# A hybrid decoder block on one core: a new order of the blocks where the MLP's first product begins, two loads moved in the DMA queue, and one place of weight preparation in attention

## The chip, the core and the metric

The kernel runs on 1 core of one Trainium2 chip. The core has TensorE (PE) for matmuls, which writes to PSUM banks of 128 x 512 f32; VectorE (DVE) and ScalarE (ACT) for elementwise work; GpSimd (POOL); and SyncE (SP), whose queue issues nearly all DMAs of this kernel. Each engine works through its own instructions in the order in which the program lists them, and waits on semaphores for the others. The metric is the device time in microseconds, the median of several runs. Before the change it is 2211.28 us.

## What is computed

A decoder block on x (1 x 1024 x 1024, f32): two parallel token mixers (retention, and dilated sliding-window attention in three groups of four heads), gates, and an MLP, each behind an RMS norm that is modulated by a condition; then a final norm.

```python
def squared_relu_mlp(h, w1, w2):
    return jnp.square(jax.nn.relu(h @ w1)) @ w2

def reference(x, c, w_ada, ...):
    for l in range(DEPTH):
        mod = jax.nn.silu(c) @ w_ada[l] + b_ada[l]
        sh1, sc1, g1, sh2, sc2, g2 = jnp.split(mod, 6, axis=-1)
        h = modulate(rms_norm(x, norm1_g[l]), sh1, sc1)
        x = x + g1[:, None, :] * token_mixer(h, w_in[l], ...)
        h = modulate(rms_norm(x, norm2_g[l]), sh2, sc2)
        x = x + g2[:, None, :] * squared_relu_mlp(h, w_ff1[l], w_ff2[l])
    return rms_norm(x, norm_f_g)
```

D_MODEL is 1024, the MLP is 4096 wide, a head has 128 channels.

## The kernel before

**Numbers.** Every f32 operand of a matmul is split into a high part (a copy by ScalarE into the matmul's type, names ending in h) and a low part (the rest, a subtraction by VectorE, names ending in l). A product is then three matmuls: low x high (L207), high x low (L209), high x high (L211), added up in one bank (mm3).

**Large products** run as 2 x 2 blocks with seven products in place of eight (class Blocks). The names of the seven in the first MLP product are 11, 12, s1, s3, s2, 22, s4; each is 12 matmuls of 128 x 512. The operands of x are 11, 21, 22 (the quarters) and t1 to t4 (their sums and differences, OPERAND). A tile pair q, of which there are NQ = 16, needs seven blocks (q, n) and four PSUM banks: bank 0 takes 11, then 12 on top of it; bank 1 takes s1, then s4; bank 2 takes s2; bank 3 takes s3, then 22. What has to be known of its methods:

- prep(q, n) makes a block's weight: for n = s1, s2, s3, s4 first a sum on VectorE (L249), then the high half on ScalarE (L254). The low half on VectorE (L264) is put off until the next prep or a flush. A weight needs a slot; most slots come back when the block's matmuls are done.
- mm(q, n) issues the 12 matmuls, and flushes the low half first if it is still open.
- post(q, n) works on the results. post(q, 11) copies bank 0 into a tile u (L286). post(q, s2) is three subtractions on VectorE: u - bank 2 (L290), v = bank 3 - u (L291), and v - bank 1 as output 22 (L1997); each output is followed by ReLU and square on ScalarE (L1998, L1999). So s4 (bank 1) and 22 (bank 3) of a q can start only behind its post(q, s2). post(q, 12), (q, 22), (q, s4) give outputs 11, 21, 12; with 21 and 12 a row of outputs is stored (f_out).
- run takes a list of blocks and issues for each: mm, then preps of coming weights as far as slots are free, a flush, post. For blocks that count as ahead (s2) post comes before the preps.

**The entry (ff1).** Half of x is normalized and split while the last steps of w_o run; so the blocks 11 of q = 0, 1 can start at once. The other half is normalized here (norm, L2047, on VectorE, with the row factors n21rb that come through TensorE), and the operands follow one after the other: t1 (L2065, then x_split, L2035 and L2036), 22 (L2038, L2039), t3 (L2079), t2 (L2088), t4 (L2105). On TensorE the blocks run (0, 11), (1, 11), (0, 12), (1, 12), (0, s1), (1, s1), (0, s3), (1, s3), (0, s2), (1, s2), and then, through run, (0, s4), (1, s4), (0, 22), (1, 22), and all blocks of q = 2, 3, and so on. a_sums (L2014 to L2019) builds two more sums of a finished q on VectorE, each pair with a store (xs_d), which the second product reads. Raw weights of q + 2 are loaded ahead of (q, 11) (w1_load).

**The second product (ff2_blocks)** goes through SEQ, seven block names for each of three chunks. Block i needs two operand tiles that b_load(i) reads back from DRAM (L2198, names b{i}0l and b{i}1l) and b_x(i, j) splits (L2184, L2180). b_load(0) is issued at (15, 11). b_load(1) is issued at the end of (15, 22), behind the store of that block's output; b_load(2) at the start of ff2_blocks, behind two loads of x1.

**Attention.** Steps has the weights of a step prepared while earlier steps run: following(s) takes what is missing of step s + 1 and the weight of step s + 2, and each preparation releases a load in SyncE's queue. A step that isn't marked manual calls following ahead of its own body. att_step(pair, i) computes keys (ak, gen runs over k = 0 to 7) and weaves something else in. For pair 1, i = 0 this is the last product of pair 0 (weave_pv): transposes of the probabilities on TensorE (L1435), their high half on ScalarE (L1439, pth) and low half on VectorE (L1440, ptl), then matmuls pv (L1459, L1460, L1461).

Of the kernel before, what the change touches and what calls it, by code (L numbers as in the profile page):

```python
# [17 lines left out]
P = 128  # L18
# [122 lines left out]
def block_kernel(ctx, tc, io, stop=None, dbg=None):  # L141
# [84 lines left out]
    class Blocks:  # L226
# [54 lines left out]
        def post(self, q, n):  # L281

            a, d, b, c = self.ps[q]
            if n == "11":
                self.t[q] = self.temps(f"{self.name}t{q}")
                nc.scalar.copy(self.t[q][0], a)  # L286
                return
            u, v = self.t[q]
            if n == "s2":
                nc.vector.tensor_sub(u, u, b)  # L290
                nc.vector.tensor_sub(v, c, u)  # L291
# [8 lines left out]
        def run(self, items, sums, before=lambda q, n: None, after=lambda q, n: None, ahead=(), rate=lambda q: 9):  # L300

            items_ahead = lambda i: i + 1 < len(items) and items[i + 1][1] in ahead
            for i, (q, n) in enumerate(items):
                before(q, n)
                self.mm(q, n)
                if n in ahead:
# [7 lines left out]
                if n not in ahead:  # L316
                    self.post(q, n)
                after(q, n)

# [626 lines left out]
        t = x4(name)  # L946
        return t.rearrange("p (a b) -> p a b", a=2)

    def a_temps(name):
        t = a_two(name)  # L950
        return t[:, 0], t[:, 1]

    def a_out(q, n, x, y=None):

# [45 lines left out]
    def queries_keys(ahead):  # L1000
        for _ in range(4):
            copy_block()
        sums = [(q, n) for q in range(NA) for n in ORDER][4:]

        def before(q, n):
            if n == ORDER[0] and q + 2 < NA:
                for part in (1, 2):
                    a_load(q + 2, part)

        turns = []  # L1010

# [20 lines left out]
        BA.run([(q, n) for q in range(NA) for n in ORDER], sums, before, after, ("s2",), lambda q: 1 if q == 0 else 2)  # L1032
        while turns:
            drain(turns.pop())
        values(ahead)
# [490 lines left out]
    def att_step(pair, i):  # L1526

        g, a = combos[i]

        def body(*args):  # L1530
            ps = ps_mm(f"ak{pair}{i}")
            gen = with_sums(proj_gen(ps, args[-1]))
            if i == len(combos) - 2:
                v_fetch(pair, 0)
            if i > 0:
                last = combos[i - 1]
                weave(gen, NK, scores_gen(pair, *last), len(SB[last[0]]), lag=2)
# [24 lines left out]
        return body  # L1562
# [319 lines left out]
    def norm_acc(x, f, key, pool):  # L1882

        n = x.shape[1]
        if f == 0:
            acc = pool.tile([P, 512], F32, tag="nacc", bufs=2, name=f"acc{key}")[:, :n]
            nc.scalar.activation(acc, x, AF.Square)
            G["acc", key] = acc
        else:
            sq = pool.tile([P, 512], F32, tag="nsq", bufs=2, name=f"sq{key}{f}")[:, :n]  # L1890
# [91 lines left out]
    def f_sums(name):  # L1982
        return G["mp"].tile([P, 2, 512], F32, tag="rl", bufs=2, name=name)

    def f_temps(name):
        return [G["mp"].tile([P, 512], F32, tag=t, bufs=2, name=name + t) for t in ("nsq", "h2t")]

    def f_out(q, n, x, y=None):

# [51 lines left out]
    def ff1(ahead):  # L2041
# [13 lines left out]
        G["rb"] = rstd_bcast(G["rs"], 0, 4, "n21")  # L2055
        BF.mm(1, "11", range(2, 4))
        BF.post(1, "11")
        BF.prep((2, "s3"))
        BF.mm(0, "12")
        BF.mm(1, "12")  # L2060
        low = None
        for m in range(4):
# [5 lines left out]
            low = x_split("t1", m, t1, None, "mh", 32)  # L2068
        norm(1)
        low()  # L2070
        BF.mm(0, "s1")
        BF.mm(1, "s1")
        lows = []
        for m in range(4):
            if m > 0:
# [6 lines left out]
            low = x_split("t3", m, t3, G["p"], "g1", 8)  # L2082

        def t2(m):
            k = 2 * m + 1
            t = t_(k, 1)
            lows[m]()
            nc.vector.scalar_tensor_tensor(t, t, mods[:, SH2 + k:SH2 + k + 1], t_(2 * m, 0), op0=ALU.add, op1=ALU.add)  # L2088
            return x_split("t2", m, t, G["p"], "g1", 8)

        for m in range(4):
# [3 lines left out]
            if m == 0:  # L2095
                BF.mm(0, "s3")
                BF.mm(1, "s3")
        low()
        BF.mm(0, "s2")
        BF.mm(1, "s2")  # L2100

        def t4(m):
            k = 2 * m + 1
            t = t_(k, 0)
            nc.vector.scalar_tensor_tensor(t, t, mods[:, SH2 + k:SH2 + k + 1], t_(k, 1), op0=ALU.add, op1=ALU.subtract)  # L2105
# [14 lines left out]
        for q in (3, 4):  # L2120
            for part in (1, 2):
                w1_load(q, part)
        for q in range(2):
            BF.post(q, "12")
        sums = [(q, n) for q in range(2, NQ) for n in ORDER]
        items = [(q, n) for n in ("s4", "22") for q in range(2)] + sums

        def before(q, n):
            if q > 2 and n == ORDER[0] and q + 2 < NQ:
# [3 lines left out]
                for f in range(3):  # L2133
                    x1_load(f + 3 * (n == "12"), x1_d)

        late = {(0, "22"): (0, 0), (2, "11"): (0, 1), (2, "12"): (1, 0), (2, "22"): (1, 1)}
        late.update({(q + 1, n): (q, part) for q in range(2, 4 * NS) for part, n in enumerate(("11", "s1"))})

        def after(q, n):
            if (q, n) in late:  # L2140
# [105 lines left out]
    def second_ahead(n):  # L2246
# [14 lines left out]
        elif n == "12":  # L2261
            for p in range(4):
                b_w(1, p)
        elif n == "22":
            b_load(1)

    def ff2_blocks(ahead):
        for i, (c, n) in enumerate(SEQ):
            if i == 0:
                b_load(2)  # L2270
                for s in range(2):
                    b_raw(0, "12", s)
            if i + 3 < len(SEQ) + 2:
# [280 lines left out]
```

## Time and profile before

| | us |
|---|---|
| median of 3 runs | 2211.28 |
| lowest and highest of them | 2211.12, 2213.42 |
| the profiled execution | 2211.89 |
| its span, from first to last instruction | 2210.1 |

So 1.8 us of the profiled execution lie around its span. The mean granted TensorE clock is 0.998. Three places of the span matter here, in us from its start: the step of attention about 1113 to 1133, the entry of the MLP from 1563 to 1650, and the beginning of the second product from 1878 to 1905.

In the timeline a row has the start, the duration, the engine, the line, the operation, the tile written, the tiles read, the shapes, and the count of instructions that were merged into the row; brackets give the engine's idle time ahead of it and what ended it. Matmuls are pipelined: their durations overlap, and what counts is the distance from start to start. Instructions of VectorE and ScalarE overlap a little too. In the view of waits a row says which engine and line waited for which engine, tile and line: us in total, how many times, the longest.

### The profile page before, as it was taken

The page shows a single profiled execution, that of the slowest core. Times are in us where ns is not written, and L with a number is a line of the kernel's source. Part 1 is how long each engine was busy: PE and PEld are TensorE (multiplying, and loading weights), DVE is VectorE, ACT ScalarE, POOL GpSimd, SP SyncE. Part 2 cuts the span into 40 slices and gives each one's busy share as a digit, 9 for nine tenths or more (in the row PEclk, how much of TensorE's full clock was granted, in tenths as well). Part 3 has the DMA queues.
Part 4 walks back from the last instruction along what each step waited for, and adds up shares of the span by engine and source line. Part 5 has one row for each costly group of instructions (what it writes and reads, how often), then busy time and mean ns, then how long its engine had stood idle before and what let it go on. Part 6 is the DMA issues. An engine that isn't in the chain of part 4 may idle for free. (4 is left out here: it accounts for less than half of the span.)

```text
span 2210.1 us, 27246 instructions
## 1 busy us (share of the span) xinstructions
PE 2174.1 (98%) x10134; PEld 1802.7 (82%) x10134; DVE 1456.5 (66%) x2284; ACT 921.8 (42%) x1689; POOL 161.0 (7%) x192
## 2 busy tenths in 40 slices
PE   7999999999999999999999999999999999999998
PEld 5888888888887888888888888888778888788887
DVE  6618777764548778865554754676876665787845
ACT  4323332223334445544644634524454445533413
POOL 0001111000012122111100000002000000000003
PEclk9999999999999999999999999999999999999999
DMA  9539999635776556557763265655244444745322
GB/s 366 201 133 280 301 289 291 193 112 181 237 269 199 176 176 206 195 169 193 175 167 96 87 252 176 239 181 161 67 159 151 146 146 183 253 134 173 122 86 77
DMA packets 156611, 408.93 MB, mean 185 GB/s; under 512 B 27446, under 2 KB 55357, under 8 KB 153278
## 3 DMA queue, kind: packets, MB, share of 16 engines
q1 hardware_dynamic: 148542, 363.14, 46.7%
q0 software_dynamic: 7936, 44.05, 9.2%
q8 instruction: 80, 1.31, 0.2%
q14 instruction: 53, 0.43, 0.1%
HBM read 316.27 MB, written 156.13 MB: 214 GB/s over the span
## 5 line engine op out<-in xcount | busy, mean ns | idle before, releaser
L207 PE MATMUL qap<-hh,qaw 128*128 128x512 f32 x216 | 84.0, 389 | 0.0
L209 PE MATMUL qap<-hl,qaw 128*128 128x512 f32 x216 | 84.0, 389 | 0.0
L211 PE MATMUL qap<-hh,qaw 128*128 128x512 f32 x216 | 84.0, 389 | 0.0
L634 POOL TENSOR_TENSOR j<-qk,j 128x512 fp32r<-128x512 f32 x32 | 43.3, 1353 | 460.5 <-ACT j L633 441.6
L1998 ACT ACTIVATE a<-a 128x512 f32<-128x512 f32 x48 | 30.3, 632 | 76.0 <-DVE a L1997 76.0
L1895 POOL TENSOR_TENSOR accnf<-accnf,sqnf 128x256 f32<-128x256 f32 (+1 forms) x18 | 16.6, 922 | 613.3 <-ACT sqnf L1891 613.3
L264 DVE TENSOR_TENSOR fw<-w1r,fw 128x512 fp32r<-128x512 f32 x48 | 32.9, 688 | 37.5 <-ACT fw L254 37.5
L1315 ACT ACTIVATE P<-P,ng 128x128 f32<-128x128 f32 (+1 forms) x96 | 42.0, 439 | 36.7 <-DVE ng L1312 36.7
L264 DVE TENSOR_TENSOR qaw<-wa,qaw 128x512 fp32r<-128x512 f32 x54 | 36.0, 685 | 30.8 <-ACT qaw L254 30.8
L2184 ACT CAST w2h<-w2s 128x512 fp32r<-128x512 f32 x36 | 22.4, 622 | 78.8 <-DVE w2s L2222 77.0
L207 PE MATMUL fp<-h2h,fw 128*128 128x512 f32 x128 | 50.0, 390 | 0.0
L209 PE MATMUL fp<-h2l,fw 128*128 128x512 f32 x128 | 49.8, 389 | 0.0
L211 PE MATMUL fp<-h2h,fw 128*128 128x512 f32 x128 | 49.8, 389 | 0.0
L207 PE MATMUL roa<-rh,rwl 128*128 128x512 f32 x128 | 49.8, 389 | 0.0
L209 PE MATMUL roa<-rl,rwh 128*128 128x512 f32 x128 | 49.8, 389 | 0.0
L211 PE MATMUL roa<-rh,rwh 128*128 128x512 f32 x128 | 49.8, 389 | 0.0
L1730 DVE TENSOR_TENSOR rwl<-rwl,rwh 128x1024 fp32r<-128x1024 f32 x25 | 30.2, 1220 | 29.1 <-ACT rwh L1760 29.1
L669 ACT COPY sm<-sT 128x128 f32<-128x128 f32 x32 | 8.5, 267 | 93.9 <-PE sT L657 93.9
L207 PEld LDWEIGHTS qap<-hh,qaw 128*128 128x128 f32 x216 | 40.5, 188 | 8.5
L209 PEld LDWEIGHTS qap<-hl,qaw 128*128 128x128 f32 x216 | 40.5, 188 | 8.4
L211 PEld LDWEIGHTS qap<-hh,qaw 128*128 128x128 f32 x216 | 40.5, 188 | 8.4
L1895 POOL TENSOR_TENSOR accn<-accn,sqn 128x512 f32<-128x512 f32 x12 | 15.5, 1294 | 392.3 <-ACT sqn L1891 392.3
(3100 smaller groups left out, 7213.6 us busy)
## 6 DMA issues: line engine op xcount, KB each, us to landing
v<-vd SPq DMA_DIRECT2D x32, 512.0 KB, 5.3
raw<-in_w_ada_dram SPq DMA_DIRECT2D x32, 512.0 KB, 4.8
w1r<-in_w_ff_dram SPq DMA_DIRECT2D x32, 512.0 KB, 5.0
vd<-vo SPq DMA_DIRECT2D x24, 512.0 KB, 6.5
yt<-y POOLq DMA_DIRECT2D x24, 512.0 KB, 6.9
xsd<-as SPq DMA_DIRECT2D x24, 512.0 KB, 2.7
w2r<-in_w_ff2s_dram SPq DMA_DIRECT2D x24, 512.0 KB, 6.9
em<-in_w_ada_dram SPq DMA_DIRECT2D x16, 512.0 KB, 10.2
```

The lines of the kernel that those rows point to most:

```text
L207: nc.tensor.matmul(o, wl, xh, start=first, stop=False, skip_group_check=skip)
L209: nc.tensor.matmul(o, wh, xl, start=False, stop=False, skip_group_check=skip)
L211: nc.tensor.matmul(o, wh, xh, start=False, stop=last, skip_group_check=skip)
L264: nc.vector.tensor_sub(t[:, 512:], src, fv(t[:, :512]))
L634: nc.gpsimd.tensor_sub(t[:, 1], src, fv(t[:, 0]))
L669: nc.scalar.copy(sm, ps[:, :C])
L1315: nc.scalar.activation(v, v, AF.Exp, bias=ng[:, blk:blk + 1], accum_out=st[:, g, blk, 2 + a:3 + a])
L1730: nc.vector.tensor_sub(lo, fv(lo), fv(hi))
L1895: (nc.vector if f == 7 else nc.gpsimd).tensor_add(G["acc", key], G["acc", key], sq)
L1998: nc.scalar.activation(o, o, AF.Relu)
L2184: nc.scalar.copy(hi, src)
```

## The change

Four edits.

1. In attention the first step of pair 1 is marked late: following isn't called ahead of its body but behind its fourth k.
2. The entry of the MLP has a new order on TensorE: ... (1, 12), (2, 11), (0, s1), (1, s1), (2, 12), (0, s3), (1, s3), (0, s2), (1, s2), (0, s4), (1, s4), (2, s1), (2, s3), (0, 22), (1, 22), (2, s2), (3, 11), (2, 22), (2, s4), (3, s1) and on as before. Nine banks would be in use, so bank 0 of q = 0, and later that of q = 2, is copied to a tile f11 by ScalarE. u has three buffers in place of two, and the tiles of post are taken one at a time. The weight of (2, 12) is prepared with that of (2, s3), ahead of the normalizations.
3. On VectorE, in the entry, t2 is built in the place of t1 and not in that of 22, so that the low halves of 22 can come behind t2, among t4 and the posts. post(0, 12) and post(1, 12) move, (q, 22) of q = 0, 1 counts as ahead, a_sums of q = 0, 1, 2 and b_load(1) go through a new hook, between, which stands behind the preps and ahead of flush and post.
4. b_load(1) is issued ahead of the store of (15, 22); b_load(2) directly behind the last block of the first product, ahead of the two loads of x1.

The diff, cut to its core:

```diff
-        def run(self, items, sums, before=..., after=..., ahead=(), rate=lambda q: 9):
+        def run(self, items, sums, before=..., after=..., ahead=lambda q, n: False,
+                rate=lambda q: 9, between=lambda q, n: None):
...
                     self.prep(sums.pop(0))
+                between(q, n)
                 if not items_ahead(i):
                     self.flush()
...
-                gen = at(gen, NK - 1, lambda: k_split(pair, g, a, ps))
+                gen = at(at(gen, 3, args[0]), NK - 1, lambda: k_split(pair, g, a, ps))
                 weave_pv(gen, NK - 1, 0, 2)
...
-                      manual=i == pair == 0)
+                      manual=("late" if pair else True) if i == 0 else False)
...
-        BF.prep((2, "s3"))
+        BF.prep((2, "s3"), (2, "12"))
         BF.mm(0, "12")
+
+        t = G["mp"].tile([P, 512], F32, tag="f11", name="f11")
+        nc.scalar.copy(t, BF.ps[0][0])
+        BF.ps[0][0] = t
         BF.mm(1, "12")
...
+        BF.mm(2, "11")
+        BF.post(2, "11")
         BF.mm(0, "s1")
         BF.mm(1, "s1")
+        BF.mm(2, "12")
...
         def t2(m):
-            k = 2 * m + 1
-            t = t_(k, 1)
-            lows[m]()
-            nc.vector.scalar_tensor_tensor(t, t, mods[:, SH2 + k:SH2 + k + 1], t_(2 * m, 0), op0=ALU.add, op1=ALU.add)
+            t = t_(2 * m, 0)
+            nc.vector.scalar_tensor_tensor(t, t_(2 * m + 1, 1), mods[:, SH2 + 2 * m + 1:SH2 + 2 * m + 2], t,
+                                           op0=ALU.add, op1=ALU.add)
...
+        lows[0]()
         low()
         BF.mm(0, "s2")
         BF.mm(1, "s2")
...
+        lows[1]()
         low = t4(0)
+        lows[2]()
+        low()
+        lows[3]()
         BF.post(0, "s2")
-        low()
         low = t4(1)
         BF.post(1, "s2")
         low()
+        BF.post(1, "12")
...
-        for q in range(2):
-            BF.post(q, "12")
-        sums = [(q, n) for q in range(2, NQ) for n in ORDER]
-        items = [(q, n) for n in ("s4", "22") for q in range(2)] + sums
+        BF.post(0, "12")
+        t = G["mp"].tile([P, 512], F32, tag="f11", name="f11b")
+        nc.scalar.copy(t, BF.ps[2][0])
+        BF.ps[2][0] = t
+        sums = [(q, n) for q in range(2, NQ) for n in ORDER if (q, n) not in ((2, "11"), (2, "12"))]
+        first_items = [(0, "s4"), (1, "s4"), (2, "s1"), (2, "s3"), (0, "22"), (1, "22"), (2, "s2"), (3, "11")]
+        items = first_items + [i for i in sums if i not in first_items]
...
-        late = {(0, "22"): (0, 0), (2, "11"): (0, 1), (2, "12"): (1, 0), (2, "22"): (1, 1)}
-        late.update({(q + 1, n): (q, part) for q in range(2, 4 * NS) for part, n in enumerate(("11", "s1"))})
+        late = {(0, "22"): (0, 0), (1, "22"): (0, 1), (2, "22"): (1, 0), (2, "s4"): (1, 1), (3, "s1"): (2, 0), (3, "s3"): (2, 1)}
+        late.update({(q + 1, n): (q, part) for q in range(3, 4 * NS) for part, n in enumerate(("11", "s1"))})
+
+        def between(q, n):
+            if q < 3 and (q, n) in late:
+                a_sums(*late[q, n])
+            if (q, n) == (2, "22"):
+                BF.post(2, "12")
+            if (q, n) == (NQ - 1, "22"):
+                b_load(1)
...
-        BF.run(items, sums[3:], before, after, ("s2",))
+        BF.run(items, sums[2:], before, after, lambda q, n: n == "s2" or n == "22" and q < 2,
+               lambda q: 1 if q == 2 else 9, between)
+        b_load(2)
         x1_load(6, x1_d)
         x1_load(7, x1_d)
...
-        elif n == "22":
-            b_load(1)
...
             if i == 0:
-                b_load(2)
                 for s in range(2):
                     b_raw(0, "12", s)
```

More of the change, by code (lines that the diff above doesn't have):

```diff
@@ L284, in post @@
             if n == "11":
-                self.t[q] = self.temps(f"{self.name}t{q}")
+                self.t[q] = [self.temps(f"{self.name}t{q}", 0)]
                 nc.scalar.copy(self.t[q][0], a)
                 return
-            u, v = self.t[q]
+            if n == "s2":
+                self.t[q].append(self.temps(f"{self.name}t{q}", 1))
+            u, v = self.t[q][0], self.t[q][-1]
             if n == "s2":
@@ L298, in post, with run @@
                 self.out(q, "12", u, d)
-        def run(self, items, sums, before=lambda q, n: None, after=lambda q, n: None, ahead=(), rate=lambda q: 9):
-            items_ahead = lambda i: i + 1 < len(items) and items[i + 1][1] in ahead
+        def run(self, items, sums, before=lambda q, n: None, after=lambda q, n: None, ahead=lambda q, n: False,
+                rate=lambda q: 9, between=lambda q, n: None):
+            items_ahead = lambda i: i + 1 < len(items) and ahead(*items[i + 1])
             for i, (q, n) in enumerate(items):
@@ L307, in run @@
                 self.mm(q, n)
-                if n in ahead:
+                if ahead(q, n):
                     self.post(q, n)
@@ L313, in run @@
                     self.prep(sums.pop(0))
+                between(q, n)
                 if not items_ahead(i):
                     self.flush()
-                if n not in ahead:
+                if not ahead(q, n):
                     self.post(q, n)
@@ L947, in a_two, with a_temps @@
         return t.rearrange("p (a b) -> p a b", a=2)
-    def a_temps(name):
-        t = a_two(name)
-        return t[:, 0], t[:, 1]
+    pairs = {}
+    def a_temps(name, i):
+        if i == 0:
+            pairs[name] = a_two(name)
+        return pairs[name][:, i]
     def a_out(q, n, x, y=None):
@@ L1030, in after @@
                 v_low(0, int(n == "22"))
-        BA.run([(q, n) for q in range(NA) for n in ORDER], sums, before, after, ("s2",), lambda q: 1 if q == 0 else 2)
+        BA.run([(q, n) for q in range(NA) for n in ORDER], sums, before, after, lambda q, n: n == "s2", lambda q: 1 if q == 0 else 2)
         while turns:
@@ L1983, in f_sums, with f_temps @@
         return G["mp"].tile([P, 2, 512], F32, tag="rl", bufs=2, name=name)
-    def f_temps(name):
-        return [G["mp"].tile([P, 512], F32, tag=t, bufs=2, name=name + t) for t in ("nsq", "h2t")]
+    def f_temps(name, i):
+        t = ("nsq", "h2t")[i]
+        return G["mp"].tile([P, 512], F32, tag=t, bufs=3 - i, name=name + t)
     def f_out(q, n, x, y=None):
@@ L2104, in t4 @@
             t = t_(k, 0)
-            nc.vector.scalar_tensor_tensor(t, t, mods[:, SH2 + k:SH2 + k + 1], t_(k, 1), op0=ALU.add, op1=ALU.subtract)
+            nc.vector.scalar_tensor_tensor(t, t, mods[:, SH2 + k:SH2 + k + 1], t_(2 * m, 0), op0=ALU.add, op1=ALU.subtract)
             return x_split("t4", m, t, A["r1"], "att", 8)
+        lows[1]()
         low = t4(0)
+        lows[2]()
+        low()
+        lows[3]()
         BF.post(0, "s2")
-        low()
         low = t4(1)
@@ L2134, in before @@
                     x1_load(f + 3 * (n == "12"), x1_d)
-        late = {(0, "22"): (0, 0), (2, "11"): (0, 1), (2, "12"): (1, 0), (2, "22"): (1, 1)}
-        late.update({(q + 1, n): (q, part) for q in range(2, 4 * NS) for part, n in enumerate(("11", "s1"))})
+        late = {(0, "22"): (0, 0), (1, "22"): (0, 1), (2, "22"): (1, 0), (2, "s4"): (1, 1), (3, "s1"): (2, 0), (3, "s3"): (2, 1)}
[7 more added lines that the diff above has]
+                b_load(1)
         def after(q, n):
-            if (q, n) in late:
+            if q > 2 and (q, n) in late:
                 a_sums(*late[q, n])
```

2 lines of the change are left out of this document (1 added, 1 removed).

## The prediction

> **What bounds the kernel now.** I read the page first, then TensorE's waits, the windows around the three places that the change touches, and the timelines there.
>
> ```profile
> PE 2174.1 (98%) x10134; PEld 1802.7 (82%) x10134; DVE 1456.5 (66%) x2284; ACT 921.8 (42%) x1689; POOL 161.0 (7%) x192
> ```
> ```profile
> PE fp L209 <- DVE xt L2036: 3.7, 4, 1.1
> ...
> PE fp L207 <- DVE ft2h2t L291: 1.5, 1, 1.5
> PE pv L1460 <- DVE ptl020(0, 0, 0)_9394 L1440: 1.2, 1, 1.2
> ...
> PE f2c L209 <- DVE b10l L2180: 0.8, 1, 0.8
> ...
> PE f2a L209 <- DVE b21l L2180: 0.4, 1, 0.4
> ```
> ```profile
> 1118.00:1126.00 8.00, 6.75 (x31) 5.36 (x30) 3.76 (x6) 2.00 (x4) 0.84 (x1) 0.79 0.91 329
> 1577.00:1605.00 28.00, 24.28 (x101) 17.86 (x100) 27.22 (x42) 14.11 (x23) 0.00 (x0) 1.00 0.21 72
> ...
> 1630.00:1650.00 20.00, 20.00 (x89) 16.30 (x88) 15.03 (x25) 9.32 (x16) 0.00 (x0) 1.00 0.55 197
> ```
>
> TensorE is busy for 98% of the span and the change takes no matmul away, so only its waits can be won. Five of them lie where the change is: two in the MLP's entry (3.7 and 1.5 us), one in attention (1.2), two where the second product begins (0.8 and 0.4). The windows (columns: length, busy time of PE, PEld, DVE, ACT, POOL, granted clock, DMA share, GB/s) add two facts: VectorE works 27.22 of 28 us in the entry, so there its queue sets the pace; and in attention the clock falls, to 0.79 on average, right at the wait.
>
> **Attention.** Rows of step 0 of pair 1:
>
> ```profile
> 1115.68 1.21 DVE L198 TENSOR_TENSOR raw_8741l<-raw,raw_8741h 128x1024 fp32r<-128x1024 f32 x1
> 1115.98 1.04 ACT L1252 ACTIVATE qh<-raw 128x1024 fp32r<-128x1024 f32 x1
> ...
> 1116.92 1.04 ACT L197 CAST raw_9294h<-raw 128x1024 fp32r<-128x1024 f32 x1
> ...
> 1117.05 1.23 DVE L1253 SCALAR_TENSOR_TENSOR ql<-raw,qh 128x1024 fp32r<-128x1024 f32 x1 [0.16 <-ACT qh L1252]
> ...
> 1117.86 0.58 ACT L1439 CAST pth020(0, 0, 0)_9393<-pt020(0, 0, 0)_9388 128x512 fp32r<-128x512 f32 x1
> ...
> 1118.19 1.22 DVE L198 TENSOR_TENSOR raw_9294l<-raw,raw_9294h 128x1024 fp32r<-128x1024 f32 x1
> ...
> 1118.49 0.33 PE L1459 MATMUL pv<-pth020(0, 0, 0)_9393,vl 128*128 128x128 f32 x1
> ...
> 1119.33 0.68 DVE L1440 TENSOR_TENSOR ptl020(0, 0, 0)_9394<-pt020(0, 0, 0)_9388,pth020(0, 0, 0)_9393 128x512 fp32r<-128x512 f32 x1
> ...
> 1120.07 0.33 PE L1460 MATMUL pv<-ptl020(0, 0, 0)_9394,vh 128*128 128x128 f32 x1 [1.25 <-DVE ptl020(0, 0, 0)_9394 L1440]
> ...
> 1122.03 1.05 PE L209 MATMUL ak<-hl,raw_8634h 128*128 128x512 f32 x2
> ```
>
> Four preparations (qh, ql and both halves of raw_9294) stand ahead of pth020 and ptl020. The change puts them, with the two loads that they release on SyncE, behind the fourth k of the step. Then pth020 can take the place of qh at 1115.98, and ptl020 follows raw_8741l at 1116.9 and ends by 1117.6, a microsecond before TensorE asks for it at 1118.6. The two matmuls L1459 and L1460 stand 1.58 us apart and would stand 0.11 apart: 1.47 us. What is late next: the four operations then run beside the k matmuls, about 3 us later; raw_9294 is the weight of the next step but one, qh that of the next step's scores, so nothing is near. If that cover failed, TensorE would wait for about 2.4 us (the two DVE rows) at a later place.
>
> The clock: 0.21 of 8 us is 1.68 us lost after the wait. I count it as won, since it fell in the microseconds after this wait and at no other place in the body. The Trainium skill (TensorE: Matmul & The Clock Gate, section "Part 1: The HAM clock gate") says the clock drops after at least one idle window of about 3.4 us; by that rule a wait of 1.25 us isn't the cause, the drop would stay, and the sum would be 1.68 us smaller. The entry's row with its four waits and a clock of 1.00 speaks for the rule, the place of the drop against it.
>
> **The MLP's entry.** I write (q, n) for a block of 12 matmuls.
>
> ```profile
> 1577.07 0.39 PE L207 MATMUL fp<-xt10h,fw0s 128*128 128x512 f32 x1
> ...
> 1586.89 0.39 PE L207 MATMUL fp<-xt,fw0s 128*128 128x512 f32 x1
> 1588.37 0.50 PE L209 MATMUL fp<-xt,fw0s 128*128 128x512 f32 x1 [1.09 <-DVE xt L2036]
> 1588.71 0.40 PE L211 MATMUL fp<-xt,fw0s 128*128 128x512 f32 x1
> ...
> 1609.93 0.39 PE L207 MATMUL fp<-h2h,fw 128*128 128x512 f32 x1
> ...
> 1620.81 0.39 PE L207 MATMUL fp<-h2h,fw 128*128 128x512 f32 x1
> ...
> 1650.03 0.39 PE L207 MATMUL fp<-h2h,fw 128*128 128x512 f32 x1
> ```
> ```profile
> 1571.88 0.59 ACT L286 COPY ft1nsq<-fp 128x512 f32<-128x512 f32 x1 [3.46 <-PE fp L211]
> 1572.36 0.62 ACT L254 CAST fw2s<-fs 128x512 fp32r<-128x512 f32 x1
> ```
> ```profile
> 1570.44 0.75 DVE L2047 SCALAR_TENSOR_TENSOR x<-x,a,n21rb 128x512 f32<-128x512 f32 x1 [1.53 <-PE n21rb L383]
> ...
> 1576.13 0.74 DVE L2047 SCALAR_TENSOR_TENSOR x<-x,a,n21rb 128x512 f32<-128x512 f32 x1
> ...
> 1578.12 0.74 DVE L2047 SCALAR_TENSOR_TENSOR x<-x,a,n21rb 128x512 f32<-128x512 f32 x1
> ...
> 1579.38 0.74 DVE L2079 SCALAR_TENSOR_TENSOR x<-x,dsh,x 128x512 f32<-128x512 f32 x1
> ...
> 1586.18 0.75 DVE L2039 SCALAR_TENSOR_TENSOR x220l<-x,mods,x220h 128x512 fp32r<-128x512 f32 x1
> ...
> 1588.23 0.75 DVE L2039 SCALAR_TENSOR_TENSOR x221l<-x,mods,x221h 128x512 fp32r<-128x512 f32 x1
> ...
> 1596.13 0.69 DVE L290 TENSOR_TENSOR ft0nsq<-ft0nsq,fp 128x512 f32<-128x512 f32 x1 [0.17 <-PE fp L211]
> ...
> 1597.58 0.69 DVE L1997 TENSOR_TENSOR a<-ft0h2t,fp 128x512 f32<-128x512 f32 x1
> ```
>
> Four blocks from 1609.93 to 1620.81 make 2.72 us a block. From (0, s1) at 1577.07 to (4, 11) at 1650.03 stand 24 blocks, 65.3 us; 72.96 went by, so 7.7 us are lost, more than the waits' 5.2, since a wait of 1.09 costs 1.48 - 0.23 and another 0.11 at the next matmul. The new order puts (2, 11) ahead of (0, s1), (2, 12) ahead of (0, s3), and (3, 11) ahead of (2, 22). I laid the three queues out in it with the starts of these rows.
>
> Against the gain stands a step of VectorE. Preparing (2, 12) there flushes the low half of (2, s3) ahead of the first normalization, and that half waits for ScalarE's fw2s, which stands behind the copy of (1, 11): done at 1572.98. So the chain of x starts at 1573.6, not 1570.44, 3.2 us late, with all of VectorE's entry behind it. On ScalarE the two f11 copies and the copies of (2, 11) and (2, 12), 0.6 us each, lie in idle time.
>
> - t1: rounds of 1.99 (1576.13 to 1578.12) end the last low half at 1582.3. (0, s1), now due 2.72 later, asks for it at 1579.79 + 10 x 0.227 = 1582.06: 0.35 us late (before, 0.2).
> - The low half of (2, 12) adds 0.6; the round of t3 takes 6.8 (1579.38 to 1586.18): its last half ends at 1591.0, asked for at 1590.7 after (0, s1), (1, s1), (2, 12): 0.4 late. Before, 0.5, 1.25 and 1.25 were lost here.
> - t2: 2.05 a round (1586.18 to 1588.23) less the 0.78 for the low half of 22, which moves behind: no wait in (0, s2), where 1.26 were lost.
> - The four low halves of 22, t4(0) and its low half now precede the three subtractions of post (0, s2) (1.45 from 1596.13 to 1597.58, and 0.69): these end at 1601.5, and (0, s4), due at 1599.8, overwrites what the third reads: 1.8 late. post (1, s2) ends at 1604.4, when (1, s4) is due.
> - From there VectorE has 23 operations (about 14.7 us at 0.64) and some 5 us of waits for ScalarE's ReLU and square pairs, until post (2, s2), whose second subtraction ends at 1625.6. (2, 22), due at 1623.5, waits for it: 2.1 late, though (3, 11) stands in between. The same at (3, 22): 0.8.
>
> With 0.11 for each restart that is 6.0 us lost, against 7.7: 1.7 won. The same layout of the old order reaches (4, 11) 0.27 early, so the layouts differ by 1.3; I take 1.5. Bounds for what the trace doesn't show (banks, slots and loads in the new order): if both long waits vanished, 4 more; if a bank or slot came 2.5 us late (one block), 2.5 fewer.
>
> **The second product's loads.**
>
> ```profile
> 1882.56 0.32 SPq L2003 DMA_DIRECT2D ad<-a  x1
> 1882.98 0.38 SPq L2198 DMA_DIRECT2D b10l<-xsd  x1
> ...
> 1888.23 1.05 ACT L2184 CAST b10h<-b10l 128x1024 fp32r<-128x1024 f32 x1 [4.51 <-DMA b10l<-xsd]
> ...
> 1890.59 0.50 PE L209 MATMUL f2c<-b10l,w2h 128*128 128x512 f32 x1 [0.76 <-DVE b10l L2180]
> ```
>
> b10l's load stands in SyncE's queue behind the store of (15, 22), which waits for the square. Ahead of it, it can go when (15, 22) frees the t4 slots, about 1876 (two blocks before the second product); the x1 loads ahead keep the engines busy, so I let it land by 1885.5, 2.7 us earlier than 1888.2, and need 1.1. Behind it wait that store and the next, whose readers come much later. b20l and b21l pass the two x1 loads. Won: 0.76 and 0.35 of idle time with 0.27 each for the restart, 1.65. If the slots come free no earlier, 0.
>
> **Sum.** 1.47 + 1.68 + 1.5 + 1.65 = 6.3 from the profiled execution's 2211.89: 2205.6. The median of the runs, 2211.28, lies 0.6 below it: **2205.0**.
>
> **Rivals.**
> - The drop of the clock isn't this wait's doing and stays (for: the entry's clock of 1.00 beside waits of 1.1 us): 1.68 us less, 2206.7. This is how the page on TensorE and its clock gate in the Trainium skill would have it.
> - The clock drops at a new place, at one of the entry's waits of 1.8 and 2.1 us, longer than any there before (against: in the entry the matmuls around them are long ones): a drop costs what it cost in attention, 2206.7.
> - The loads win nothing, since slots or the x1 loads hold them: 2206.7. Against: half of the idle interval would do.
> - The entry goes better: VectorE's operations after 1604 find gaps that I filled with waits, and the long waits go: 2201 to 2203.
> - Slower: the late post recurs. The wait of 1.5 us at (2, 22), 1.8 with its restart, came from a post queued behind sums and preparations on VectorE. If the new order left VectorE so far behind that each of the 13 remaining q had it, 23 us: 2228; from four of them the change is slower. Against: from q = 3 on the order is the old one, and from 1630 to 1650 VectorE has 5 us of 20 free (15.03 busy), with TensorE busy for all 20.
>
> **Chances.** Forecast 0.52, drop stays 0.13, drop at a new place 0.07, loads 0.08, entry better 0.13, late posts 0.05, the remainder two of the small losses together. A change of 0.2%, 4.4 us, is about what a measurement here can tell from none: faster needs under 2206.9, so the forecast counts almost wholly, the clock and loads cases for half: faster 0.76, same 0.19, slower 0.05. The range takes the better entry's near half and the sum without the clock and with a block lost in the entry (2205.0 + 1.7 + 2.5): 2201.8 to 2209.2.
>
> **What would show it.** Right: no wait of pv L1460 on ptl020 near 1119, and a clock of 1.00 there; norm at L2047 starting 3 us after n21rb; waits of TensorE on DVE L1997 and L291 of about 1.8 and 2.1 us at (0, s4) and (2, 22), none on the t2 halves; b10l's load ahead of the store, and no wait on b10l or b21l. Wrong: waits on a PSUM bank at (2, s1) or (2, s3), a wait of VectorE for a store or a load after (3, 11), a drop of the clock in the entry, or waits at each (q, 22).

## The result, and the profile after

| us | before | after |
|---|---|---|
| median (10 runs of each) | 2211.20 | 2205.95 |
| lowest and highest | 2209.74, 2213.56 | 2204.85, 2207.17 |
| profiled execution | 2211.89 | 2205.88 |
| its span | 2210.1 | 2204.1 |

The ratio is 0.9976, 95% interval 0.9968 to 0.9985: faster by 5.25 us, where 6.3 from the profiled execution was forecast. The two profiled executions differ by 6.0. Some of that is chance, as the experiments show.

The page's row of busy times, and TensorE's waits in the changed kernel (waited for by which line and tile: us in total, times, longest):

```profile
PE 2170.8 (98%) x10134; PEld 1802.6 (82%) x10134; DVE 1456.4 (66%) x2284; ACT 922.9 (42%) x1691; POOL 161.1 (7%) x192
```
```profile
PE fp L207 <- DVE ft2h2t L293: 2.6, 1, 2.6
...
PE fp L207 <- DVE a L2005: 1.6, 1, 1.6
...
PE fp L207 <- DVE ft3h2t L293: 0.6, 1, 0.6
...
PE fp L207 <- DVE ft15h2t L293: 0.5, 1, 0.5
...
PE fp L209 <- DVE xt L2044: 0.2, 1, 0.2
PE fp L209 <- DVE xt13l L2044: 0.2, 1, 0.2
```

TensorE's share stays at 98%. The waits on ptl020, b10l and b21l are gone, and of the 3.7 us for the halves of x (L2036 before, L2044 now) 0.2 is left. In their place stand two waits for the first post of a pair, at (0, s4), 1.6 and at (2, 22), 2.6, a smaller one at (3, 22), and one that was not forecast: (15, 22), at the end of the first product.

A window (length; busy time of PE, PEld, DVE, ACT, POOL; granted clock; DMA share; GB/s) and, in the next fence, the rows of pv:

```profile
1118.00:1126.00 8.00, 8.00 (x55) 7.17 (x53) 4.25 (x5) 2.85 (x4) 0.84 (x1) 1.00 0.97 293
```
```profile
1117.25 1.06 ACT L1259 ACTIVATE qh<-raw 128x1024 fp32r<-128x1024 f32 x1
...
1117.97 0.22 PE L1466 MATMUL pv<-pth020(0, 0, 0)_9381,vl 128*128 128x128 f32 x1
...
1118.03 0.27 PE L1467 MATMUL pv<-ptl020(0, 0, 0)_9382,vh 128*128 128x128 f32 x1
```

The first two pv stand 0.06 us apart, 1.58 before; qh now starts behind the split that they need; 55 matmuls go through the 8 us where 31 went, at a clock of 1.00 where it was 0.79.

Where the 6.0 us between the two spans lie, from the starts of three matmuls in each trace (the first of n21ss, the first of the second product, the first of nf2ss):

| us | before | after | gain |
|---|---|---|---|
| up to n21ss (retention, attention) | 1565.89 | 1562.21 | 3.68 |
| n21ss to the second product | 312.62 | 312.42 | 0.20 |
| second product | 322.27 | 320.11 | 2.16 |
| the rest | 9.35 | 9.33 | 0.02 |

The entry itself does better than the second row says: from n21ss to (4, 11) it takes 83.13 us (1562.21 to 1645.34), 84.14 before (1565.89 to 1650.03). The wait at (15, 22) takes 0.77 of that gain of 1.0 back.

### The profile page after: what moved, and what is told of

Same layout as the page of the kernel before. It is cut to its first block, busy times and chain, and to the rows that moved or that the text cites. A ratio compares the mean times of both kernels' runs of the same rounds, so it can differ in the third digit from the quotient of the medians.

```text
span 2204.1 us, 27245 instructions
## 1 busy us (share of the span) xinstructions
PE 2170.8 (98%) x10134; PEld 1802.6 (82%) x10134; DVE 1456.4 (66%) x2284; ACT 922.9 (42%) x1691; POOL 161.1 (7%) x192
```

## The experiments

Three theories were on trial: that attention's wait caused the drop of the clock; that VectorE's late start and the queue ahead of post (2, s2) make what the entry still loses; and, for the new wait at (15, 22), that the entry or the loads made it. Losses below are how much later than its normal step the matmul started; they add 0.16 to the idle time of the row, and 0.11 more follows at the next matmul. Each ratio is against the kernel before, run on the same chip.

### One part of the change at a time

The kernel before with one of the three parts. Attention alone:

```diff
-                gen = at(gen, NK - 1, lambda: k_split(pair, g, a, ps))
+                gen = at(at(gen, 3, args[0]), NK - 1, lambda: k_split(pair, g, a, ps))
...
-                      manual=i == pair == 0)
+                      manual=("late" if pair else True) if i == 0 else False)
```

> The kernel before with the attention edit alone (the preparations behind the fourth k of the step). Theory: the wait of 1.25 us on ptl020 causes the drop of the clock, so both go: 1.47 + 1.63 = 3.1 us, to 2208.1. Rival: the clock drops for another reason (a rule of 3.4 us of idle time would need a longer wait): the drop stays within some microseconds of 1121, and the gain is 1.5, to 2209.7. Both: no wait on ptl020, entry and second product as before.

Measured: 2208.53 us (11 runs), before 2210.72; ratio 0.9990, 0.9982 to 0.9999. The wait is gone, and so is the drop behind it. But the drop isn't gone from the kernel. Windows of its profile:

```profile
1118.00:1126.00 8.00, 8.00 (x52) 7.04 (x51) 4.25 (x6) 3.48 (x4) 0.84 (x1) 1.00 0.90 267
1581.40:1584.82 3.42, 1.71 (x6) 0.76 (x5) 3.35 (x6) 1.50 (x3) 0.00 (x0) 1.00 0.00 0
1584.82:1588.23 3.41, 2.94 (x7) 2.37 (x8) 3.34 (x6) 1.09 (x2) 0.00 (x0) 0.50 0.00 0
```

The clock is 0.50 from 1584.82 to 1588.23, in the old entry, behind a stretch of the same length in which TensorE was busy for half. Neither theory had said that: the drop stands at another place.

The entry alone (the changed kernel without the edits to attention and to b_load):

> The kernel before with the new order of the MLP's entry alone. Theory: waits in the entry as in the changed kernel, 0.35 at (0, s1), 0.36 at (0, s3), 1.8 at (0, s4), 2.7 at (2, 22), 0.8 at (3, 22), so 6.5 us lost there against 7.5 before: a gain of 1.0, to 2210.2; the wait on ptl020 and the drop of the clock to a half for 3.4 us behind it are there. The new wait of 0.5 us at (15, 22): if the new order of the entry makes it, it is here; if the earlier loads make it, it is not; if it comes from how long b00l's load takes (6.1 us from issue to its copy in the changed kernel, 4.6 before), it is here only if that load takes more than about 5.3 us.

Measured: 2210.36 us (11 runs), before 2210.72; ratio 0.9998, 0.9990 to 1.0007. The waits of TensorE up to (2, 22) are those of the changed kernel within 0.05 us; (3, 22) and (15, 22) have none. Attention's wait of 1.25 us is there, but no drop behind it, where the expectation had one; the drop is behind (2, 22), where it also explains (3, 22): TensorE comes there later, and the post is done.

```profile
1119.44:1122.85 3.41, 2.50 (x17) 2.28 (x18) 2.05 (x4) 0.25 (x1) 0.84 (x1) 1.00 0.89 326
1122.85:1126.27 3.42, 3.42 (x25) 3.07 (x24) 0.69 (x1) 0.59 (x1) 0.00 (x0) 1.00 1.08 304
1621.20:1624.61 3.41, 1.10 (x5) 0.56 (x3) 3.38 (x6) 1.69 (x3) 0.00 (x0) 1.00 0.91 337
1624.61:1628.03 3.42, 3.16 (x8) 2.49 (x9) 2.12 (x5) 2.43 (x5) 0.00 (x0) 0.50 0.89 314
```

The loads alone:

```diff
+        def between(q, n):
+            if (q, n) == (NQ - 1, "22"):
+                b_load(1)
...
+        b_load(2)
         x1_load(6, x1_d)
...
-        elif n == "22":
-            b_load(1)
...
             if i == 0:
-                b_load(2)
```

> The kernel before with the earlier loads of b10l, b11l, b20l and b21l alone. Theory: the waits on b10l, b11l and b21l go, 2.06 us with their restarts, to 2209.1, and attention keeps its wait and the drop of its clock. Rival: slots or the x1 loads hold them and nothing is won. The wait of 0.5 us at (15, 22): here, if these loads make it (then the gain is 1.3, to 2209.9).

Measured: 2209.27 us (11 runs), before 2210.72; ratio 0.9991, 0.9982 to 1.0000. No wait for b10l, b11l or b21l is left, and the second product takes 320.11 us from its first matmul to nf2ss, as in the changed kernel, where before took 322.27 and 321.92 in two profiles: 1.8 to 2.2 us won. Attention's wait passes without a drop here too; its clock drops in the entry:

```profile
1583.53:1586.94 3.41, 1.25 (x5) 0.48 (x3) 3.37 (x6) 1.91 (x3) 0.00 (x0) 1.00 0.00 0
1586.94:1590.36 3.42, 3.42 (x8) 2.75 (x9) 3.35 (x6) 0.62 (x1) 0.00 (x0) 0.50 0.00 0
```

A wait at (15, 22) is there, 0.6 us. But attention alone, which has neither the loads nor the entry, has one too, of 0.28. What the executions with it share is a long load of b00l. Rows of the kernel before, then of the loads alone:

```profile
1863.93 0.37 SPq L2198 DMA_DIRECT2D b00l<-xsd  x1
...
1868.49 1.05 ACT L2184 CAST b00h<-b00l 128x1024 fp32r<-128x1024 f32 x1 [2.44 <-DMA b00l<-xsd]
```
```profile
1862.60 0.37 SPq L2205 DMA_DIRECT2D b00l<-xsd  x1
...
1868.78 1.05 ACT L2191 CAST b00h<-b00l 128x1024 fp32r<-128x1024 f32 x1 [3.89 <-DMA b00l<-xsd]
1869.87 1.23 DVE L2187 TENSOR_TENSOR b00l<-b00l,b00h 128x1024 fp32r<-128x1024 f32 x1 [4.17 <-ACT b00h L2191]
1871.72 0.69 DVE L291 TENSOR_TENSOR ft15h2t<-fp,ft15nsq 128x512 f32<-128x512 f32 x1
...
1872.47 0.50 PE L207 MATMUL fp<-xt,fw 128*128 128x512 f32 x1 [0.59 <-DVE ft15h2t L291]
```

Post (15, s2) stands on VectorE behind the low half of b00l, which waits for the load by way of ScalarE. From issue to copy the load took 4.56 us here and 6.18 there. Over the profiles with this order of work: 4.56, 5.12, 5.13, 5.53 and 5.57 without a wait; 5.72 (0.13 us of wait), 5.75 (0.15), 5.84 (0.24), 5.89 (0.28), 6.10 (0.50) and 6.18 (0.59). From about 5.6 us on, what the load takes longer TensorE waits longer. In the same kernel the load varies: 6.10, 5.84 and 5.13 in three profiles of the changed one.

### The late start of VectorE's chain

Rows of the changed kernel, VectorE and ScalarE, where the chain of x begins:

```profile
1568.21 0.59 ACT L286 COPY ft1nsq<-fp 128x512 f32<-128x512 f32 x1 [3.45 <-PE fp L211]
...
1568.70 0.62 ACT L254 CAST fw2s<-fs 128x512 fp32r<-128x512 f32 x1
...
1569.35 0.69 DVE L264 TENSOR_TENSOR fw2s<-fs,fw2s 128x512 fp32r<-128x512 f32 x1 [4.12 <-ACT fw2s L254]
...
1569.96 0.74 DVE L2055 SCALAR_TENSOR_TENSOR x<-x,a,n21rb 128x512 f32<-128x512 f32 x1
...
1570.88 0.59 ACT L2070 COPY f<-fp 128x512 f32<-128x512 f32 x1 [1.04 <-PE fp L211]
...
1571.46 0.62 ACT L2043 CAST xt10h<-x 128x512 fp32r<-128x512 f32 x1
```

This is the step as forecast: the copy of (1, 11), then fw2s, its low half, and only then norm. The first experiment takes the two preparations ahead of that copy:

```diff
         BF.post(0, "11")
+        BF.prep((2, "s3"), (2, "12"))
         BF.mm(1, "11", range(2))
...
         BF.post(1, "11")
-        BF.prep((2, "s3"), (2, "12"))
```

> The changed kernel with the preparations of (2, s3) and (2, 12) emitted ahead of the copy of (1, 11), so that ScalarE makes fw2s some 3 us earlier and VectorE's chain starts when n21rb is there. Theory: the 3.2 us of late start are masked by a second gate, the f11 copy, which waits on ScalarE for the end of (0, 12) ahead of the halves of t1: norm starts 3.1 us earlier, but the low half of t1 waits about 2.5 us, and only 0.6 us is won: no wait at (0, s1), 0.2 at (0, s3), still 1.6 at (0, s4) and 2.5 at (2, 22). Rival: the late start is the only gate; then the waits at (0, s1), (0, s3) and (0, s4) all go: 2.7 us. The clock: windows of 3.413 us on a fixed grid, and a drop to a half for the next 3.413 us behind a window in which TensorE idles for 1.7 us or more; the wait at (2, 22) brings one in about three of four executions. Rival on the clock: a drop follows the longest wait wherever the grid lies.

Measured: 2205.47 us (9 runs), before 2210.90; ratio 0.9974, 0.9965 to 0.9984: next to the changed kernel's. Rows of VectorE (filtered to it), then of ScalarE:

```profile
1566.56 0.75 DVE L2055 SCALAR_TENSOR_TENSOR x<-x,a,n21rb 128x512 f32<-128x512 f32 x1 [0.75 <-PE n21rb L387]
...
1571.81 0.69 DVE L2044 TENSOR_TENSOR xt10l<-x,xt10h 128x512 fp32r<-128x512 f32 x1 [2.39 <-ACT xt10h L2043]
```
```profile
1570.67 0.59 ACT L2070 COPY f<-fp 128x512 f32<-128x512 f32 x1 [2.08 <-PE fp L211]
```

The norm starts when n21rb is there, 3.4 us earlier, and 2.39 of it is lost again at the first low half: the f11 copy holds ScalarE's queue until (0, 12) is through. The waits at (0, s1) and (0, s3) are gone; (0, s4) and (2, 22) keep 1.6 and 2.6. So there are two gates in a row, and the second was hidden by the first. With both opened:

```diff
         BF.mm(0, "12")
-        t = G["mp"].tile([P, 512], F32, tag="f11", name="f11")
-        nc.scalar.copy(t, BF.ps[0][0])
-        BF.ps[0][0] = t
...
             low = x_split("t1", m, t1, None, "mh", 32)
+            if m == 1:
+                t = G["mp"].tile([P, 512], F32, tag="f11", name="f11")
+                nc.scalar.copy(t, BF.ps[0][0])
+                BF.ps[0][0] = t
```

> As the kernel with the earlier preparations, and the f11 copy behind the second half of t1 on ScalarE. Theory: with both gates gone the waits at (0, s1), (0, s3) and (0, s4) go, 2.7 us with their restarts, and 2.3 to 2.6 at (2, 22) and 0.6 at (3, 22) stay: 2206.0 - 2.8 = 2203.2. Rival: a bank or VectorE's queue behind the chain keeps (0, s4) waiting: under 1.3 won.

Measured: 2202.77 us (5 runs), before 2210.90; ratio 0.9961, 0.9947 to 0.9974. No wait at (0, s1), (0, s3) or (0, s4); of those in the entry this row of its waits is all that is left ((3, 22) has none, since the clock drops behind (2, 22) in this execution):

```profile
PE fp L207 <- DVE ft2h2t L293: 2.4, 1, 2.4
```

The late start was what the entry's first three waits came from, once the second gate is counted with it.

### What stands ahead of post (2, s2)

VectorE's queue in the changed kernel up to the first subtraction of post (2, s2); (2, 22) waits for the second:

```profile
1618.09 0.68 DVE L2005 TENSOR_TENSOR a<-fp,ft1nsq 128x512 f32<-128x512 f32 x1
1618.69 0.68 DVE L249 TENSOR_TENSOR fs<-fs,w1r 128x512 f32<-128x512 f32 x1
1619.29 0.68 DVE L264 TENSOR_TENSOR fw3s<-fs,fw3s 128x512 fp32r<-128x512 f32 x1
1619.89 0.68 DVE L2026 TENSOR_TENSOR as<-a,a 128x512 f32<-128x512 f32 x1
1620.49 0.68 DVE L2027 SCALAR_TENSOR_TENSOR as<-as,a 128x512 f32<-128x512 f32 x1
1621.09 0.68 DVE L292 TENSOR_TENSOR ft2nsq<-ft2nsq,fp 128x512 f32<-128x512 f32 x1
```

A preparation and a pair of sums, 2.4 us, stand between post (1, 22) and post (2, s2), none of them urgent. The experiment puts the sums behind the two subtractions, here and for q = 3:

```diff
         if ("out", q) not in M:
+            if q in (2, 3):
+                a_sums(q - 2 + (q == 3), 1)
             M["out", q] = ...
...
-        late = {(0, "22"): (0, 0), (1, "22"): (0, 1), (2, "22"): (1, 0), (2, "s4"): (1, 1), (3, "s1"): (2, 0), (3, "s3"): (2, 1)}
+        late = {(0, "22"): (0, 0), (2, "22"): (1, 0), (2, "s4"): (1, 1), (3, "s1"): (2, 0)}
```

> The changed kernel with the sums over q = 0 and q = 2 (second part) placed between the subtractions of post (2, s2) and post (3, s2) and their outputs, not ahead of them. Theory: the two subtractions start 1.2 us earlier, so the wait at (2, 22) falls from 2.6 to 1.4 and that at (3, 22), 0.6, goes: 2.0 us, and no wait of this kernel fills 1.7 us of a clock window, so that the drop that the changed kernel has in some executions there goes too: 2203.0 to 2204.0. Rival: what is late is the preparations and ScalarE's pairs ahead of them, and (2, 22) keeps over 2 us.

Measured: 2205.02 us (7 runs), before 2210.90; ratio 0.9973, 0.9962 to 0.9983. From its waits:

```profile
PE fp L207 <- DVE a L2007: 1.6, 1, 1.6
PE fp L207 <- DVE ft2h2t L293: 1.4, 1, 1.4
...
PE fp L207 <- DVE ft3h2t L293: 0.5, 1, 0.5
```

(2, 22) fell by the 1.2 us of the two sums, as expected; (3, 22) did not go, since TensorE now comes there 1.2 us sooner and VectorE's queue does not. So the time came out 1 us above the expected 2203.0 to 2204.0. From n21ss to the second product, less the loss at (15, 22), this profile takes 310.59 us, where the changed kernel's first took 311.65; neither has a drop of the clock on that way. All of it together, and the split of b01 behind post (15, s2) (b_x(0, 1) at block s2 in place of s3):

> The changed kernel with earlier preparations, the f11 copy behind the second half of t1, the two sums behind the subtractions, and the split of b01 behind post (15, s2). Theory: the entry loses 1.5 us or less, against 6.5; no wait at (15, 22); no drop of the clock in the body in any execution, since no window holds 1.7 us of idle time: 2206.0 - 2.8 - 2.0 - 0.6, and 1.2 for the clock: 2199.6, with a smaller spread of its runs than the kernel before (2209.6 to 2212.5). Rival: the clock drops once wherever the waits lie, and the edits share one gate: 2202 to 2203.

Measured: 2201.97 us (5 runs, 2201.10 to 2203.39), before 2210.90; ratio 0.9959, 0.9946 to 0.9971, the fastest kernel here. The entry's waits:

```profile
PE fp L207 <- DVE ft2h2t L293: 1.2, 1, 1.2
...
PE fp L207 <- DVE ft3h2t L293: 0.4, 1, 0.4
```

With restarts 2.2 us are lost, not 1.5; n21ss to the second product takes 307.48, 312.42 in the changed kernel. The expectation of 2199.6 was 2.4 too low. 0.7 of it is this; the clock term, put at 1.2, was some 0.8 too high (below), and the 0.6 for (15, 22) had been counted for every execution, though not every one has that wait. What is left isn't told from chance. In the profile the load of b00l took 5.01 us, with which no other profile has a wait, so that the moved split of b01 shows nothing.

### The clock

In each trace the change of clock comes a whole number of windows of 3.413 us after the clock's first rise in that execution (in the kernel before 1099.09 us after it, 322 windows; in attention alone 1559.89, 457). The windows laid end to end from that rise are called the grid here; each execution has its own. The next four runs ask whether the drop follows the work inside one window of that grid. Three are repeats:

> The changed kernel once more, for a second look at its clock. Theory of the grid: its waits are the same, and the clock drops behind the wait of 2.6 us at (2, 22) in 6 of 10 executions, according to where the windows lie; when it does, the execution is 1.6 us longer. Rival (the change took the drop away with attention's wait): no drop in the body in any execution.

> The changed kernel a third time: as for the second look. On (15, 22): a wait there if b00l's load takes 5.7 us or more from its issue to its copy, none if under 5.5.

> The kernel before once more. Theory of the grid: the same waits, and the drop of the clock is where the windows put it: behind attention's wait, or behind the waits at (0, s3), or nowhere in the body in about two of ten executions. Rival (attention's wait is the cause): behind attention's wait again.

Measured: 2206.58 and 2206.22 us for the changed kernel, 2209.95 for the one before, one run each. The windows around (2, 22), in the changed kernel's first profile, its second and its third:

```profile
1617.66:1621.07 3.41, 2.32 (x11) 1.58 (x9) 3.41 (x6) 1.77 (x3) 0.00 (x0) 1.00 0.85 314
1621.07:1624.48 3.41, 1.93 (x8) 1.61 (x9) 2.69 (x5) 1.20 (x3) 0.00 (x0) 1.00 0.96 323
1624.48:1627.90 3.42, 3.42 (x17) 2.82 (x15) 2.77 (x5) 2.47 (x6) 0.00 (x0) 1.00 0.48 151
```
```profile
1619.94:1623.35 3.41, 1.09 (x5) 0.91 (x6) 3.34 (x6) 0.76 (x2) 0.00 (x0) 1.00 0.92 335
1623.35:1626.76 3.41, 3.41 (x10) 2.67 (x9) 2.14 (x5) 2.42 (x6) 0.00 (x0) 0.50 0.49 172
```
```profile
1619.62:1623.04 3.42, 0.89 (x4) 0.48 (x3) 3.35 (x6) 0.95 (x2) 0.00 (x0) 1.00 0.92 340
1623.04:1626.45 3.41, 3.41 (x9) 2.68 (x9) 2.14 (x5) 2.78 (x5) 0.00 (x0) 0.50 0.68 232
```

The wait is the same 2.5 to 2.6 us in all three. In the first the border of two windows cuts it, TensorE is busy for 2.32 and 1.93 us on either side, and nothing happens; in the others one window holds nearly all of it, and the clock is 0.50 in the next: 10 and 9 matmuls of the first product go through where 17 went. At (15, 22) the second profile has a wait of 0.24, the third none. The kernel before, taken again, has its wait in attention and no drop anywhere in the body:

```profile
1117.04:1120.46 3.42, 2.17 (x12) 1.50 (x11) 3.29 (x4) 2.48 (x5) 0.84 (x1) 1.00 0.39 119
1120.46:1123.87 3.41, 3.41 (x24) 3.01 (x24) 0.87 (x2) 0.33 (x1) 0.00 (x0) 1.00 1.02 347
```

And the combined kernel with attention's edit undone. The wait of 1.2 us at (2, 22) is in it too, but attention's is the only one around which a window can hold less than 0.38 of full streaming, counted as below:

> The combined kernel with the attention edit undone, so that the wait of 1.25 us on ptl020 is the only place in the body where a window of 3.413 us can have TensorE below some 0.4 of full streaming. Theory (the drop follows such a window on a fixed grid): every execution loses the wait's 1.5 us, and the executions whose grid puts the wait well inside one window lose 1.6 us more, between a third and a half of them: times in two groups, about 2203.5 and 2205.1. Rival (this wait always brings the drop): all at 2202.0 + 3.1 = 2205.1. Rival (the drop comes once, whatever waits there are): then the combined kernel has it too, and this one is 1.5 slower.

Measured: 2203.32 us (5 runs: 2202.39, 2202.65, 2203.32, 2204.24, 2205.19), before 2211.10; ratio 0.9961, 0.9948 to 0.9975. The profiled run is the longest:

```profile
1118.66:1122.07 3.41, 2.16 (x16) 1.67 (x15) 3.20 (x5) 1.38 (x3) 0.84 (x1) 1.00 0.77 250
1122.07:1125.49 3.42, 3.42 (x12) 2.74 (x12) 0.00 (x0) 0.00 (x0) 0.00 (x0) 0.50 1.07 298
```

The runs spread over 2.8 us, as the theory of the grid has it, though not in two clean groups. By the differences to before, this kernel is 1.15 us behind the combined one (7.78 won for 8.93); that is less than the 2.0 that the edit is worth by the account below, and within what medians of five leave open. That the drop follows attention's wait always is refuted by the entry alone, the loads alone and the repeat of before; that it comes once in any case, by the profiles of the combined kernel and of the one with the sums moved, whose bodies have none.

Busy time alone doesn't order these windows: 2.16 (drop) and 2.17 (none), and above, 1.93 in the changed kernel's first profile (none). It counts a matmul of 128 columns like a long one. If each matmul is counted by its columns instead, with 0.227 us (the step of the 128 x 512 ones) for 512, the windows at full clock of all 13 profiles sort cleanly, some 8200 of them up to the end of the second product:

```
share of the window   followed by a drop
0.18 0.23 0.25 0.28 0.28 0.33 0.34 0.34   all eight, in eight executions
0.43 0.45 0.46 0.46 0.46 0.47 ...          none
```

The two attention windows with 2.16 us busy (in the kernel before and here) come to 0.33 and 0.34 (16 matmuls, most of them of 128 columns), the one of 2.17 to 0.46. At the end of the span, around the last norm, every execution has one more drop, behind windows of 0.07 to 0.30; one window there of 0.41 (both gates opened, 2190.23 to 2193.64) has none behind it. The last four runs were made with some 0.4 as the expected threshold; the figures on either side of it were read off afterwards, from the windows that they sort.

## Why the prediction was right, point by point

**The time** came out 1 us above the forecast of 2205.0 and inside the range. Attention's wait and the loads were right; the entry came out smaller, and the clock term fitted one profile, in part by luck, and was wrong as a cause.

**Attention** held: 1.52 us gone between the two matmuls (1.58 to 0.06) for 1.47, the four preparations beside the k matmuls, no wait in their place. Alone the edit won 2.2 us by medians.

**The clock** is the step that failed: "I count it as won, since it fell in the microseconds after this wait and at no other place in the body." The 1.68 us were indeed absent from the changed kernel's first profile, but by luck as well as by this edit: there a border of the grid cut the wait at (2, 22), and the second and third profile have the drop behind it. Attention's wait was one of several that can bring the drop, and whether one does changes with the grid of each execution. An estimate, by sliding a window with a threshold of 0.38 over the traces: before, 0.32 of the positions of the grid have the drop in attention and 0.41 in the entry; after, 0.60 have it at (2, 22). With thresholds from 0.35 to 0.41 these are 0.24 to 0.49, 0.34 to 0.68 and 0.54 to 0.66. The 13 profiles agree as far as so few can: the drop is there in two of the five with attention's wait, in two of the four with the old entry, and in four of the six with the wait of 2.4 us and more at (2, 22).

Nor does a drop always cost its 1.6 us. In attention it does: n21ss is reached at 1565.89 with it and at 1564.32 without, in the two profiles of before. In front of another wait on VectorE much of it is absorbed: from n21ss to the second product, less the loss at (15, 22), the changed kernel took 311.65 us without the drop, and 312.36 and 312.27 with it, 0.6 to 0.7 more: the wait at (3, 22), 0.76 and its restart, is then gone. In the old entry it costs 0.1: 312.71 and 312.72 with it (attention alone, the loads alone), 312.62 and 312.59 without (the two profiles of before). So the edit in attention is worth 0.32 x 1.57 = 0.5 beside its 1.5, and the new wait at (2, 22) gives 0.60 x 0.65 = 0.4 of it back.

The prediction's argument against the rival "the drop stays", the place of the drop, was a coincidence of one profile, and the rival "The clock drops at a new place, at one of the entry's waits" is what two profiles of three show, though at 0.65 and not at the full price that it was given. The Trainium skill (TensorE: Matmul & The Clock Gate, section "Part 1: The HAM clock gate") has a free-running window of 3413 ns, and the trace agrees with 3.413 us; its "after ≥1 idle window" doesn't fit: no window ahead of a drop was idle throughout, and they held up to 0.34 of full streaming.

**The entry** won 1.0 us against 1.5. The waits at (0, s1), (0, s3), (0, s4) and (3, 22) came as worked out: lost 0.32, 0.36, 1.78 and 0.76 for 0.35, 0.4, 1.8 and 0.8; t2 waits gone. The mis-sized term is (2, 22): 2.73 for 2.1. Its mechanism was right: sums and preparations ahead of post (2, s2). The late start was right at 3.2 us, but only one of two gates: "the two f11 copies ... lie in idle time" held just because the start was late; without it the first of them is the gate.

**The second product's loads** won 1.8 to 2.2 us for 1.65. b10l's load was issued ahead of the store, and its copy starts 6.3 us after the second product's first matmul, where the forecast's 1885.5 meant 7.0 (the product began at 1878.51 before, at 1874.63 after):

```profile
1880.89 1.05 ACT L2216 CAST b10h<-b10l 128x1024 fp32r<-128x1024 f32 x1 [1.58 <-DMA b10l<-xsd]
```

That is 4.6 us ahead of the first use of b10h, which in the changed kernel is at 1885.51. The wait on b11l, a loss of 0.24 and 0.11 for the restart, had not been counted.

**Not forecast** was (15, 22), 0.77 in the profiled execution. It is not the change's: attention alone has it without the entry and the loads, and the kernel before lacked it with a load of b00l of 4.56 us. What makes that load long in one execution and short in another stays open.

**The sum.** Of the 5.25 that the medians differ by, these terms explain 4.6: attention 1.5 + 0.5, entry 1.0 - 0.4, loads 2.0. By medians the parts alone won 2.2, 0.4 and 1.5, each uncertain by about 2 us. The forecast's 6.3 had 1.6 too much for the clock and 0.5 too much for the entry, and 0.35 too little for the loads. The 0.65 that is left can be chance: two profiles of one kernel differ by as much (TensorE's wait for the state of retention, which the change doesn't touch, was 1.0 us in the profile before and 0.5 in the one after).

## What to carry to other kernels

Before a stall is credited with a drop of the clock, take a second profile: if the drop lands elsewhere, its price belongs to all waits that can bring it, weighted by how often, and it goes only when the last of them is short enough. When an engine's chain starts late, look for the next gate behind the first before pricing the repair: here the first alone won about as much as the measurement can tell from nothing, and both together 3.2 us (2205.95 to 2202.77). And an operation that reads a DMA, placed ahead of a result that TensorE needs, turns the spread of that load into the spread of the kernel.

## What the hardware showed that was not expected

A wait of 1.25 us among matmuls of 128 columns can halve the clock for 3.413 us (in two profiles of five), while one of 2.6 us among long matmuls may pass without a drop, if a border of the grid falls into it (in two of six). In these 13 profiles the threshold lies between 0.34 and 0.41 of full streaming in one window. And the same load in the same kernel took 5.13, 5.84 and 6.10 us to its first reader in three executions.
